# A decoder trunk on one core: the second feed-forward matrix set between whole blocks of the first, and weight buffers handed on by age

## The chip, the cores and the metric

The kernel runs on one core of a Trainium2 chip. The metric is the device time of one execution in microseconds (us). Before the change it was 2306.26 us, the median of three runs from 2303.05 to 2313.5 us.

## What is computed

The reference is a trunk of two layers on 512 tokens of width 1024. Each layer projects the normalised input once (`h @ w_in`), runs four causal token mixers on pieces of it, gates and sums their outputs, and then does this:

```
x  = x + mixed @ w_out
h2 = rms_norm(x, norm_ff)
x  = x + square(relu(h2 @ w_ff1)) @ w_ff2
```

`w_out` is 1024 x 1024, `w_ff1` 1024 x 4096 and `w_ff2` 4096 x 1024. The change lies in these three lines and in the buffers that their weights pass through. All matmuls read float32 data as a pair of a rounded part and a remainder, three matmuls for each product.

## The kernel before, in words

**Stages.** For each layer `mix` runs the four mixers in an order written out by hand, and `feed` runs the three lines above: first the output projection (eight weight chunks, in `OUT_ORDER`), then `factors`, which prepares the normalised input, then the feed-forward part.

**Blocks.** The hidden width of 4096 is cut into eight blocks of 512, n = 0 to 7. Each block is a 2 x 2 product done with seven products in place of eight (Strassen and Winograd). Its weights are four loaded quarters, "11", "21", "22" and "12" (512 KB each), and four sums of them that DVE makes: s3 = 21 + 11, s1 = 21 + 22 (written over 21), s2 = s3 + 22 and s4 = s2 + 12. Each of the seven weights 11, s3, s2, 12, s1, s4, 22 is then split: ACT copies it to a rounded tile, and DVE subtracts the copy and writes the remainder in place. `quarters` traces all this. One product is 24 matmuls of 256 columns. Its order on the tensor engine (PE), as traced, is 11; then s4 and 22 of the block before (`finish`, which also squares the hidden values); then s3, s2, 12, s1. So the last two products of a block lie in the block after it.

**Groups of the second matrix.** `down` multiplies the hidden values of two blocks by eight chunks of `w_ff2` (m = 0 to 7, 24 matmuls of 512 columns each, 512 KB each). It is called inside blocks 2, 4 and 6, after `finish`, and once more behind block 7. The first two chunks are begun with half of their matmuls each (`first`), since the hidden values of the second block come late.

**Weight buffers.** `chunk` and `quarters` load into 4 KB-per-partition buffers that hold the raw weight and later its remainder. `mix` uses three of them, wr0 to wr2, in turn (`dual("wr")`). `feed` uses nine: these three and ww3 to ww8, which share memory with the mixers' tiles `yl` and `e`. They stand in a list, `wfree`: `take` pops its head, `drop` appends a buffer behind the last product that reads it. Both happen while the program is traced, so which buffer a load gets is fixed by program order, and at run time the load waits until the last reader of that buffer is done. A block holds seven of the nine. The list lives on from one layer to the next.

**Tiles for the rounded copies.** `wh` has two slots and serves the chunks and the weights s3 and s1 of a block; `fh` has three and serves 11, s2, 12, s4 and 22. The hidden values take `fx`, eight slots, four for each block.

**What sets the order.** A planner puts the instructions of each engine into a fixed order at compile time: by priority, each as soon as the planner's own model says that it is ready. Loads, sums and splits of weights are traced at a priority 2000 instructions ahead of their place (`high_priority(2000)`), evacuations of blocks 4000 ahead. All weight loads are issued on SP's queue, which works in order.

The lines that the steps of the prediction touch are the split on lines 580 to 584, the sums on lines 589 to 598, the loads on lines 577 (quarters) and 301 (chunks), the split of a chunk on lines 305 and 306, and the copies of the mixers' sum on lines 497 and 498.

Of the kernel before, what the change touches and what calls it, by code (L numbers as in the profile page):

```python
# [10 lines left out]
F32R = mybir.dt.float32r  # L11
# [33 lines left out]
def fb(ap):  # L45
    return ap.bitcast(F32)


class Dual:
# [5 lines left out]
    @property  # L55
    def f(self):
        assert self.live
        return self._f
# [6 lines left out]
class Kern:  # L65
# [50 lines left out]
    def take(self):  # L116

        b = self.wfree.pop(0)
        if b[2] is not None:
            b[2].live = False  # L120
        b[2] = Dual(b[0], b[1])
        b[2].home = b
        return b[2]

    def drop(self, d):
        d.live = False
        self.wfree.append(d.home)
# [318 lines left out]

    def mix(self, l, x):
        nc = self.nc
        self.l = l
        if l > 0:  # L450
            self.load_small(l)
        self.hh, self.hl = self.norm_split(x, self.sp(l, C_GMIX, 8))

        p0 = self.tc.cur_priority
        acc = [self.vproducts("s") for _ in range(2)]
        with self.tc.high_priority(self.tc.cur_priority - p0):
            self.rb, self.rt = self.rms(x, "d", l == 0)
        if l == 0:
            self.setup_more()
        else:  # L460
            for k in range(KT):
                nc.sync.dma_start(self.xs[:, k, :], x[k][:])
        for c in range(2):
            self.sb_v(c, acc[c])
        self.dtag = "d"
        self.mixed, self.begun = None, set()
        self.y, self.Ab, self.st, self.cd, self.gg, self.V = {}, [None] * 4, {}, {}, {}, {}
        gens = {}
        for it in MIXERS:
            f = getattr(self, it[0])  # L470
            if it[0] in STEPS:
                g = gens.get(it[:-1])
                if g is None:
                    g = gens[it[:-1]] = f(*it[1:-1])
                next(g, None)
            else:
                f(*it[1:])
        assert all(next(g, self) is self for g in gens.values())
# [9 lines left out]

    def feed(self, l):
        nc = self.nc  # L490
        X2 = lambda tiles: lambda k: tiles[k // 2][:, (k % 2) * S:(k % 2) * S + S]
        HH, HL = [], []
        for k in range(0, KT, 2):
            hh, hl = self.t("fx", 1024, F32R), self.t("fx", 1024, F32R)
            for i in range(2):
                h = slice(i * S, i * S + S)
                nc.scalar.activation(hh[:, h], self.mixed[k + i][:], AF.Copy)
                nc.vector.tensor_sub(hl[:, h], self.mixed[k + i][:], fb(hh[:, h]))
            HH.append(hh)
            HL.append(hl)  # L500
        x = self.load_x(self.A["x"] if l == 0 else self.xs)
        for m in OUT_ORDER:
            wh, wl = self.chunk(wide=True)
            o = self.ps("d")
            self.halves(wh, wl, X2(HH), X2(HL), o[:], range(KT))
            self.drop(wl)
            with self.hi():
                nc.vector.tensor_add(x[m][:], x[m][:], o[:])
        F = self.factors(x, self.sp(l, C_GFF, 8))
        pend, hid = None, []  # L510
        for n in range(8):
            W = self.quarters()
            s = dict(W=W, X=self.ps("s"), H=hid)
            self.product(s["X"], W["11"], F["11"], True)
            s["e1"] = self.taken(s["X"])
            if pend:
                self.finish(pend, F)
            if n > 0 and n % 2 == 0:
                self.down(x, hid[:4], None)
                del hid[:4]  # L520
            if n == 1:
                ms, rs = self.square_norm(x)
                for k in range(KT):
                    nc.vector.tensor_mul(x[k][:], x[k][:], ms[:])
            if n == 0:
                s["Z"] = self.ps("s")
                self.product(s["Z"], W["12"], F["21"], True)
            s["Y"] = self.ps("s")
            self.product(s["Y"], W["s3"], F["3"], True)
            self.product(s["X"], W["s2"], F["2"], False)  # L530
            s["e2"] = self.taken(s["X"])
            if n > 0:
                s["Z"] = self.ps("s")
                self.product(s["Z"], W["12"], F["21"], True)
            s["ra"], s["rb"] = self.t("rl", 1024), self.t("rl", 1024)
            with self.evac():
                nc.vector.tensor_add(s["ra"][:, 0:S], s["Z"][:], s["e1"][:])
                nc.scalar.activation(s["ra"][:, 0:S], s["ra"][:, 0:S], AF.Relu)
            self.product(s["X"], W["s1"], F["1"], False)
            with self.evac():  # L540
                e3 = self.taken(s["Y"])
                nc.vector.tensor_add(s["rb"][:, S:], s["X"][:], e3[:])
            pend = s
        self.down(x, hid, rs, pend, F, l == self.depth - 1)
        return x
# [23 lines left out]
    def quarters(self):  # L569

        nc = self.nc
        q, out = {}, {}
        add = nc.vector.tensor_add

        def load(n):
            q[n] = self.take()
            nc.sync.dma_start(q[n].f[:], self.A["w"][self.cidx])
            self.cidx += 1

        def split(n):  # L580
            wh = self.t("wh" if n in ("s3", "s1") else "fh", 1024, F32R)
            nc.scalar.activation(wh[:], q[n].f[:], AF.Copy)  # L582
            nc.vector.tensor_sub(q[n][:], q[n].f[:], fb(wh[:]))
            out[n] = wh, q[n]
        with self.tc.high_priority(2000):
            for n in QUARTERS[:3]:
                load(n)
            q["s3"] = self.take()
            add(q["s3"].f[:], q["21"].f[:], q["11"].f[:])
            split("11")  # L590
            q["s1"] = q["21"]
            add(q["s1"].f[:], q["21"].f[:], q["22"].f[:])
            q["s2"] = self.take()
            add(q["s2"].f[:], q["s3"].f[:], q["22"].f[:])
            split("s3")
            load("12")
            q["s4"] = self.take()
            add(q["s4"].f[:], q["s2"].f[:], q["12"].f[:])
            for n in ("s2", "12", "s1", "s4", "22"):
                split(n)  # L600
        return out

    def factors(self, x, gcol):

# [858 lines left out]
def _kxm(w, c0):  # L1463

    k = w.shape[0] // P
    return w[:, c0:c0 + P].reshape(k, P, P).transpose(1, 0, 2).reshape(P, k * P)
# [11 lines left out]
QUARTERS = ("11", "21", "22", "12")  # L1478
# [21 lines left out]
def weight_stream(inp, l):  # L1500
    w = inp["w_in"][l]
    out = []
# [35 lines left out]
    for m in OUT_ORDER:  # L1538
        out.append(_kxm(inp["w_out"][l], m * P))

    def quarters(n):
        for q in QUARTERS:
            i, j = int(q[0]) - 1, int(q[1]) - 1
            c = n * 512 + i * 256
            out.append(inp["w_ff1"][l][j * 512:(j + 1) * 512, c:c + 256].reshape(4, P, 256).transpose(1, 0, 2)
                       .reshape(P, 1024))
    for n in range(9):
        if n < 8:
            quarters(n)
        if n > 0 and n % 2 == 0:  # L1550
            g = n // 2 - 1
            for m in (0, 2, 1, 3, 4, 5, 6, 7) if n == 8 else range(8):
                out.append(_kxm(inp["w_ff2"][l][g * 1024:(g + 1) * 1024], m * P))
    return out


# [74 lines left out]
```

## Time and profile before

| | us |
|---|---|
| median of three runs | 2306.26 |
| lowest and highest | 2303.05, 2313.5 |
| the profiled execution | 2308.0 |
| its span, first to last instruction | 2306.3 |
| around the span | 1.7 |
| PE busy in the span | 2219.8 (96%) |
| DVE busy | 1638.6 (71%) |
| ACT busy | 1148.0 (50%) |

The profiled execution lies 1.7 us above the median and inside the range of the runs. Layer 0's `feed` runs from about 736 to 1154 us of the span, layer 1's from about 1876 us to the end. The share of busy time of PE says little by itself, since matmuls overlap and a slow one counts as busy; what counts is how many matmuls a stretch holds.

### The profile page before, as it was taken

The page shows a single profiled execution, that of the slowest core. Times are in us where ns is not written, and L with a number is a line of the kernel's source. Part 1 is how long each engine was busy: PE and PEld are TensorE (multiplying, and loading weights), DVE is VectorE, ACT ScalarE, POOL GpSimd, SP SyncE. Part 2 cuts the span into 40 slices and gives each one's busy share as a digit, 9 for nine tenths or more (in the row PEclk, how much of TensorE's full clock was granted, in tenths as well). Part 3 has the DMA queues.
Part 4 walks back from the last instruction along what each step waited for, and adds up shares of the span by engine and source line. Part 5 has one row for each costly group of instructions (what it writes and reads, how often), then busy time and mean ns, then how long its engine had stood idle before and what let it go on. Part 6 is the DMA issues. An engine that isn't in the chain of part 4 may idle for free.

```text
span 2306.3 us, 31559 instructions
## 1 busy us (share of the span) xinstructions
PE 2219.8 (96%) x11896; PEld 1876.3 (81%) x11896; DVE 1638.6 (71%) x2577; ACT 1148.0 (50%) x1773; POOL 398.6 (17%) x743
## 2 busy tenths in 40 slices
PE   8999999998998999999999999999989999999997
PEld 7888888886787898887888888788768878988886
DVE  6889597888864775464558886878888558663645
ACT  5775444445444553353447654434455446442433
POOL 1223124433111000000112220334431110000000
PEclk9999999999899999999999999999989999999999
DMA  4222223321124122223222222223211342223231
GB/s 164 77 72 74 83 74 96 124 85 55 55 92 146 65 93 92 96 88 103 103 95 70 70 70 90 73 96 122 78 55 57 102 143 74 101 83 110 76 108 46
DMA packets 63119, 204.91 MB, mean 89 GB/s; under 512 B 7496, under 2 KB 10184, under 8 KB 62968
## 3 DMA queue, kind: packets, MB, share of 16 engines
q1 hardware_dynamic: 62968, 202.90, 26.7%
q8 instruction: 95, 1.56, 0.3%
q14 instruction: 56, 0.46, 0.1%
HBM read 198.57 MB, written 4.29 MB: 88 GB/s over the span
## 4 chain that ended last, share of the span: by engine, by line
PE 87%; DVE 7%; ACT 2%; DMA 2%; issue 1%; POOL 1%; POOLq 0%; DVEq 0%; SPq 0%; ACTq 0%
PE pd L147 60%; PE ps L147 26%; PE ps L975 1%; DMA wr0f<-in_w 1%; DVE wr1r L306 0%; ACT fh L582 0%; ACT wh L582 0%; DMA ww7f<-in_w 0%; POOL sm L858 0%; DVE sh L1089 0%; DVE wr0r L306 0%; ACT wh L305 0%; DVE fx L674 0%; DVE Q L861 0%; DMA wr2f<-in_w 0%
## 5 line engine op out<-in xcount | busy, mean ns | idle before, releaser
L147 PE MATMUL pd<-hh,wh 128*128 128x512 f32 x1040 | 416.0, 400 | 0.8 <-DVE gt L407 0.8
L147 PE MATMUL pd<-fx,wh 128*128 128x512 f32 (+1 forms) x1264 | 400.2, 394 | 12.4 <-ACT wh L305 12.3
L147 PE MATMUL pd<-hl,wh 128*128 128x512 f32 x1040 | 411.0, 395 | 0.0
L147 PEld LDWEIGHTS pd<-fx,wh 128*128 128x128 f32 x1264 | 238.4, 190 | 63.8 <-ACT wh L305 15.8
L147 PE MATMUL ps<-F,fh 128*128 128x256 f32 x1280 | 246.7, 284 | 21.2 <-ACT fh L582 21.1
L147 PEld LDWEIGHTS pd<-hh,wh 128*128 128x128 f32 x1040 | 195.6, 188 | 45.7 <-issue 4.2
L147 PEld LDWEIGHTS pd<-hl,wh 128*128 128x128 f32 x1040 | 195.4, 188 | 41.9 <-issue 0.2
L147 PEld LDWEIGHTS ps<-F,fh 128*128 128x128 f32 x1280 | 205.5, 191 | 27.1 <-ACT fh L582 23.0
L726 DVE TENSOR_TENSOR x<-x,pd 128x512 f32<-128x512 f32 (+1 forms) x63 | 42.8, 679 | 192.4 <-PE pd L147 192.4
L305 ACT ACTIVATE wh<-wr0f 128x1024 fp32r<-128x1024 f32 x77 | 81.6, 1060 | 150.0 <-PE pd L147 128.6
L147 PE MATMUL pd<-hh,wr2r 128*128 128x512 f32 x392 | 154.2, 393 | 0.0
L305 ACT ACTIVATE wh<-wr2f 128x1024 fp32r<-128x1024 f32 x72 | 76.3, 1059 | 125.3 <-PE pd L147 106.0
L147 PE MATMUL pd<-hh,wr1r 128*128 128x512 f32 x336 | 132.7, 395 | 0.0
L305 ACT ACTIVATE wh<-wr1f 128x1024 fp32r<-128x1024 f32 x68 | 72.0, 1059 | 109.3 <-PE pd L147 85.8
L147 PE MATMUL pd<-hh,wr0r 128*128 128x512 f32 x312 | 122.8, 394 | 0.0
L147 PE MATMUL ps<-p,v 128*128 128x384 f32 (+3 forms) x384 | 116.2, 426 | 2.7 <-POOL p L878 2.7
L306 DVE TENSOR_TENSOR wr0r<-wr0f,wh 128x1024 fp32r<-128x1024 f32 x77 | 100.9, 1310 | 22.1 <-ACT wh L305 21.6
L147 PE MATMUL pd<-yh,wh 128*128 128x512 f32 x256 | 104.0, 406 | 9.9 <-ACT yh L737 9.1
L147 PE MATMUL ps<-F,wh 128*128 128x256 f32 x512 | 108.3, 299 | 3.2 <-ACT p L553 1.9
L878 POOL TENSOR_SCALAR_AFFINE_SELECT p<-p 128x128 f32<-128x128 f32 x192 | 81.7, 445 | 160.3 <-ACT p L877 158.7
L781 POOL TENSOR_TENSOR mixed<-mixed,gt 128x512 f32<-128x512 f32 x48 | 66.8, 1396 | 245.4 <-DVE gt L779 241.8
L306 DVE TENSOR_TENSOR wr2r<-wr2f,wh 128x1024 fp32r<-128x1024 f32 x72 | 96.3, 1338 | 12.3 <-ACT wh L305 11.8
(636 smaller groups left out, 5522.6 us busy)
## 6 DMA issues: line engine op xcount, KB each, us to landing
wr0f<-in_w SPq DMA_DIRECT2D x91, 512.0 KB, 3.4
wr1f<-in_w SPq DMA_DIRECT2D x84, 512.0 KB, 3.3
wr2f<-in_w SPq DMA_DIRECT2D x80, 512.0 KB, 3.3
ww7f<-in_w SPq DMA_DIRECT2D x22, 512.0 KB, 3.4
ww6f<-in_w SPq DMA_DIRECT2D x20, 512.0 KB, 3.4
ww3f<-in_w SPq DMA_DIRECT2D x18, 512.0 KB, 3.3
ww5f<-in_w SPq DMA_DIRECT2D x16, 512.0 KB, 3.4
ww8f<-in_w SPq DMA_DIRECT2D x13, 512.0 KB, 3.4
```

The source lines that it names most:

```text
L147: i = self.nc.tensor.matmul(o, l, r, start=start, stop=stop, skip_group_check=True)
L305: nc.scalar.activation(wh[:], raw.f[:], AF.Copy)
L306: nc.vector.tensor_sub(raw[:], raw.f[:], fb(wh[:]))
L726: nc.vector.tensor_add(x[m][:, h], x[m][:, h], o[:, 0:h.stop - h.start])
L781: nc.gpsimd.tensor_add(self.mixed[m][:], self.mixed[m][:], g)
L878: nc.gpsimd.affine_select(d[:, 0:P], d[:, 0:P], [[1, P]], OP.is_gt if strict else OP.is_ge, 0.0, base=0, channel_multiplier=-1)
L975: nc.tensor.transpose(S3[n][:, c:c + P], at(F, q)[:, j * P:(j + 1) * P], self.ident)
```

## The change

Four things change.

1. `quarters` becomes a generator in two parts. Part one loads 11, 21 and 22, makes s3 and s1 and splits 11. Part two makes s2, loads 12, makes s4 and splits the other six.
2. `down` moves. It is called in blocks 3, 5 and 7, between the two parts of `quarters`, before any product of the block; the last call behind block 7 stays. It reads the hidden values of the two blocks that ended before the block just past (in block 3: blocks 0 and 1). The order of the weights in memory follows.
3. The tiles of the rounded copies are dealt out in another way: `wh` serves s3, 12 and s4 beside the chunks, `fh` serves 11, s2, s1 and 22.
4. `widen`, at the start of `feed`, puts the three wr buffers at the head of the list, the one that `mix` used longest ago first. `narrow`, at the start of `mix`, lets `mix` begin its turn with the wr buffer that was freed first.

```diff
+    def narrow(self):
+        wr = [b for b in self.wfree if b in self.ring["wr"][1]]
+        self.ring["wr"] = [0, wr]
+    def widen(self):
+        n, wr = self.ring["wr"]
+        n %= len(wr)
+        self.wfree = wr[n:] + wr[:n] + [b for b in self.wfree if b not in wr]
...
     def mix(self, l, x):
         nc = self.nc
+        self.narrow()
...
     def feed(self, l):
         nc = self.nc
+        self.widen()
...
         for n in range(8):
-            W = self.quarters()
+            prep = self.quarters()
+            W = next(prep)
+            if n > 2 and n % 2:
+                self.down(x, hid[:4], None)
+                del hid[:4]
+            next(prep)
             s = dict(W=W, X=self.ps("s"), H=hid)
             self.product(s["X"], W["11"], F["11"], True)
             s["e1"] = self.taken(s["X"])
             if pend:
                 self.finish(pend, F)
-            if n > 0 and n % 2 == 0:
-                self.down(x, hid[:4], None)
-                del hid[:4]
...
-            wh = self.t("wh" if n in ("s3", "s1") else "fh", 1024, F32R)
+            wh = self.t("wh" if n in ("s3", "12", "s4") else "fh", 1024, F32R)
...
             add(q["s1"].f[:], q["21"].f[:], q["22"].f[:])
+        yield out
+        with self.tc.high_priority(2000):
             q["s2"] = self.take()
             add(q["s2"].f[:], q["s3"].f[:], q["22"].f[:])
-            split("s3")
             load("12")
             q["s4"] = self.take()
             add(q["s4"].f[:], q["s2"].f[:], q["12"].f[:])
-            for n in ("s2", "12", "s1", "s4", "22"):
+            for n in ("s3", "s2", "12", "s1", "s4", "22"):
                 split(n)
-        return out
+        yield out
```

The function that lays out the weights in memory puts quarters 11, 21, 22 ahead of a group of `w_ff2` and quarter 12 behind it, in blocks 3, 5 and 7.

## Rows read from the trace of the kernel before

**Rows 1.** The page: engines' shares of the chain that ended last.

```profile
PE 87%; DVE 7%; ACT 2%; DMA 2%; issue 1%; POOL 1%; POOLq 0%; DVEq 0%; SPq 0%; ACTq 0%
```

**Rows 2.** PE's waits over the span: total us, times, longest us.

```profile
PE ps L147 <- ACT fh L582: 21.1, 9, 4.8
PE pd L147 <- ACT wh L305: 12.3, 7, 6.6
```

**Rows 3.** Windows of 20 us: busy us and instructions per engine, PE's granted clock.

```profile
807.00:827.00 20.00, 20.00 (x170) 20.00 (x169) 18.39 (x21) 14.79 (x18) 0.00 (x0) 1.00 0.31 103
...
899.00:919.00 20.00, 16.02 (x105) 15.19 (x104) 16.49 (x16) 8.30 (x11) 0.00 (x0) 0.83 0.17 53
990.50:1010.50 20.00, 16.09 (x119) 15.52 (x118) 17.42 (x17) 12.09 (x14) 0.00 (x0) 0.91 0.27 93
1081.50:1101.50 20.00, 16.03 (x112) 15.32 (x113) 14.24 (x14) 8.27 (x11) 0.00 (x0) 0.91 0.38 122
2036.50:2056.50 20.00, 15.72 (x112) 15.04 (x112) 17.34 (x17) 9.24 (x12) 0.00 (x0) 0.91 0.21 63
2127.00:2147.00 20.00, 14.62 (x100) 14.12 (x99) 15.85 (x15) 10.73 (x13) 0.00 (x0) 0.83 0.23 79
2219.50:2239.50 20.00, 15.99 (x117) 15.30 (x116) 15.10 (x14) 11.87 (x14) 0.00 (x0) 0.91 0.43 139
```

**Rows 4.** The chain of waits behind block 4's group: start us, us, what.

```profile
985.12 5.10 PE pd L147 x23
990.22 3.35 DMA ww5f<-in_w
...
993.59 1.23 DVE ww8f L592
...
997.09 1.15 DVE ww4r L583
...
998.28 29.88 PE ps L147 x234
```

**Rows 5.** SP's timeline in block 2's group: issues of block 3's quarters.

```profile
846.44 0.33 SPq L577 DMA_DIRECT2D ww3f<-in_w  x1
...
887.83 0.33 SPq L577 DMA_DIRECT2D ww8f<-in_w  x1
...
898.82 0.33 SPq L577 DMA_DIRECT2D wr0f<-in_w  x1
```

**Rows 6.** The two seams from `mix` to `feed`: windows, columns as in rows 3.

```profile
735.90:762.00 26.10, 19.38 (x72) 15.34 (x72) 9.38 (x11) 8.27 (x11) 1.57 (x1) 0.80 0.37 131
1876.50:1900.00 23.50, 19.16 (x73) 15.27 (x74) 9.51 (x12) 8.22 (x11) 1.58 (x1) 0.85 0.40 145
```

**Rows 7.** SP's timeline at layer 0's seam, chunk loads into wr buffers.

```profile
724.75 0.33 SPq L301 DMA_DIRECT2D wr1f<-in_w  x1
...
735.74 0.33 SPq L301 DMA_DIRECT2D wr0f<-in_w  x1
```

**Rows 8.** The chain of waits at layer 1's seam.

```profile
1879.06 0.43 ACT fx L497
...
1879.59 2.00 ACT wh L305 x2
```

**Rows 9.** The chain in layer 0's output projection: one chunk.

```profile
780.18 5.50 PE pd L147 x24
```

**Rows 10.** SP's timeline there: the load of block 0's quarter 22.

```profile
756.92 0.33 SPq L577 DMA_DIRECT2D wr1f<-in_w  x1
```

**Rows 11.** ACT's timeline there: splits of a chunk, of s2, of quarter 22.

```profile
762.65 1.06 ACT L305 ACTIVATE wh<-ww4f 128x1024 fp32r<-128x1024 f32 x1 [3.09 <-PE pd L147]
...
769.17 1.06 ACT L582 ACTIVATE fh<-ww3f 128x1024 fp32r<-128x1024 f32 x1
...
797.66 1.06 ACT L582 ACTIVATE fh<-wr1f 128x1024 fp32r<-128x1024 f32 x1
```

**Rows 12.** A window inside block 4's group, columns as in rows 3.

```profile
947.00:987.00 40.00, 40.00 (x195) 33.56 (x194) 13.34 (x15) 9.26 (x9) 0.00 (x0) 1.00 0.30 99
```

More of the change, by code (lines that the diff above doesn't have):

```diff
@@ L1539, in weight_stream, with quarters @@
         out.append(_kxm(inp["w_out"][l], m * P))
-    def quarters(n):
-        for q in QUARTERS:
+    def quarters(n, qs):
+        for q in qs:
             i, j = int(q[0]) - 1, int(q[1]) - 1
@@ L1548, in weight_stream @@
         if n < 8:
-            quarters(n)
-        if n > 0 and n % 2 == 0:
+            quarters(n, QUARTERS[:3])
+        if n > 2 and (n % 2 or n == 8):
             g = n // 2 - 1
@@ L1553, in weight_stream @@
                 out.append(_kxm(inp["w_ff2"][l][g * 1024:(g + 1) * 1024], m * P))
+        if n < 8:
+            quarters(n, QUARTERS[3:])
     return out
```

## The prediction, made before the change was run

> **What bounds the kernel now.** I read the page's chain first: 87% of it is PE [rows 1], so time comes from making PE stand still less or run faster, not from fewer instructions elsewhere. Then PE's waits: its two largest groups are waits for a split weight, behind ACT's copy on line 582 (a quarter) and line 305 (a chunk) [rows 2]. Those lie in the feed-forward stage and at its start. So I went through that stage in windows. Where nothing is wrong, 20 us hold 170 matmuls of 256 columns at the full granted clock [rows 3]. Behind each of the six groups of `w_ff2` that lie inside the blocks (three in each layer), a window of the same length holds only 105, 119, 112, 112, 100 and 117 [rows 3]. The reader should see two things in these rows: the missing matmuls, and a granted clock of 0.83 to 0.91. [...]
>
> The chain behind one group says why [rows 4]. The group's last chunk ends at 990.22. At that moment, and no sooner, a quarter of the next block is issued; it lands after 3.35 us, then DVE adds, splits, and the steady row of matmuls begins at 998.28. The load is late because of the list of buffers, not because of the queue: block 3's four quarters go out at 846.44, 887.83, 898.82 and one between the last two [rows 5]. These three are 5.5 us apart, which is just one chunk's time on PE [rows 9]. When `quarters(3)` is traced, the head of `wfree` holds the three buffers through which the eight chunks were passed in turn, so 11, 21 and 22, which everything else in the block rests on, wait for the chunks' last readers. Quarter 12, needed last, got a buffer that had long been free, and went out 41 us sooner. Nothing is left to cover the wait: the planner has by then used up the last two products of the block before, which are traced behind 11, as fill inside the group: 40 us inside a group hold 195 matmuls [rows 12], where chunks alone would be 40 / 0.229 = 175 (0.229 us is 5.50 us over 24 [rows 9]).
>
> The second place is the seam from the mixers to the output projection. From the mixers' last matmul, 26.1 us hold 72 matmuls of 512 columns in layer 0, 23.5 us hold 73 in layer 1 [rows 6]. In layer 0 the three wr buffers come free 5.5 us apart, wr1 at 724.75 and wr0 last, at 735.74 [rows 7], and the first chunk was given wr0. In layer 1 the first chunk sits in ww7, mixer memory, and its split stands on ACT behind the last copy of `mixed` [rows 8].
>
> **What the change takes away.** Groups: at full pace six windows would hold 6 x 170 = 1020 matmuls; they hold 665. The 355 missing ones are 355 x 20 / 170 = 41.8 us. Seams, at 0.229 us a matmul: layer 0, 26.1 - 72 x 0.229 = 9.6 us; layer 1, 23.5 - 73 x 0.229 = 6.8 us. Together 16.4. All in all at most 58.2 us.
>
> **What becomes of the groups, followed through the list.** In block 2 the list is empty once all seven weights are taken. Behind it come, in order of their drops, the buffers of 11, of block 1's s4 and 22, then s3, s2, 12 and s1 of block 2. Part one of `quarters(3)` takes the first four, all free before the group starts. The chunks get the other three in turn (s2's, 12's, s1's). Part two gets them back: s2 the sixth chunk's buffer, free two chunks (11 us) before the group ends, quarter 12 the seventh's, 5.5 us before, s4 the last. Quarter 12 thus lands 5.5 - 3.35 = 2.1 us before the end. Its `wh` slot may come from the last chunk; then 1.06 us on ACT [rows 11] and 1.23 on DVE [rows 4] make it ready 2.3 us behind the group. Ahead of it PE has s3 and s2, 24 matmuls each, 2.8 us by the steady pace, 5.6 us in all. On ACT and DVE the hidden values of the block before come first, since `fx` is full until the group ends: two copies and two subtractions, 2 x 1.23 on DVE behind the first copy. That makes 4.7 us instead of 2.3, still under 5.6. So the stall at the end goes. What is late next is s4, which is not needed until the next block.
>
> At the group's start the first chunk's load waits for s2, lands 3.35 us later and is split in 2.3: 5.6 us, while 12 and s1 run 5.6. The fill, should it be late, is 11 of block 3, and s4 and 22 of block 2: three products of 2.8 us, 8.5 in all, that are ready. The second chunk needs a `wh` slot while s4 and the first chunk hold both; when the planner runs out of chunk work it has to run s4, which frees one. Its split (2.3 us) lies under 22 (2.8). Inside a group PE is full now with 3 buffers and 2 slots [rows 12], and stays so. I take 0.5 us for each group, 3 us, as what small waits remain; the ends are 0 and the second rival's price.
>
> **Seams.** Layer 0's first chunk gets wr1, free 11 us before the mixers end, and a `wh` slot with the second to last chunk of `mix`, 5.5 us before; its split takes 2.3. Layer 1 is the same with its oldest wr buffer. What could take over is `mixed`: its last tile is copied from 1879.06 on [rows 8]; copy and subtraction of 512 columns take half of a split's 1.06 and 1.23 us by estimate, so it is there at about 1880.3. It feeds the last three of the first chunk's 24 matmuls, due 21 x 0.229 = 4.8 us after the chunk begins at 1876.5, so at 1881.3. I take 0.5 us each, 1 us; ends 0 and 2 us each, should it come late.
>
> **Edits costed near nothing.** Matmuls, loads and splits are the same in number; each is only moved, on SP's queue past the chunks' loads as well. Quarter 12 of block 0 now waits for a `wh` slot of the last output chunk (it had `fh`), and s1 moves to `fh`. ACT at the end of the projection does one copy for the other, 1.06 us. Cover: 11 of block 0 runs for about as long; without it up to 2.3 us a layer. I take 0.5 each, 1 us. `narrow` only turns the names: `mix` of layer 1 starts on buffers that are released one by one before the layer begins, as now. DVE is the engine to watch, 18.39 of 20 us in steady blocks [rows 3], but there PE is already full.
>
> Sum: 2308.0 (span 2306.3 and 1.7 around it) - 58.2 + 3 + 1 + 1 = 2254.8. The profiled execution stands 1.7 us over the median, so I forecast **2253 us** for the median.
>
> **Rivals.**
> First, the change does only half of what it says: the planner again pulls 11, s3 and s2 of the next block into the group as fill, and quarter 12 is missed just as 22 is now. The fill in today's order [rows 12] speaks for it; against it that 12 now goes out one chunk before the end and that s2 cannot be used before the sixth chunk. Then only the seams gain: 2308 - 16.4 + 2 = 2293, 2292 for the median.
>
> Second, the stall moves to the group's start: ACT works in order, and the second chunk's split stands at its head until s4 is done, with evacuations behind it. One split shows, 2.3 us, and the lower clock behind it; at the layer 0 seam 9.6 us were lost, and PE's longest wait behind line 305 was 6.6 [rows 2], so a factor of 1.45: 3.3 us, times six, 20 us: 2273. ACT's waits for PE before a chunk's split [rows 11] speak for it, the 8.5 us of fill against it. [...]
>
> Third, slower: s3 of the next block, ready early, takes one of the two `wh` slots before the chunks do. Its remainder may not be written until s2's sum has read it, and that waits for the sixth chunk's buffer. The chunks then pass through one slot, and five of them show 2.3 x 1.45 = 3.3 us each, 16.5 a group, 99 in all: 2253 + 99 = 2352; 8.5 us of fill a group, 51 in all, bring it down to about 2300. It decides from 58.2 / 6 = 9.7 us a group, that is three chunks that show. Against it: block 0's quarter 22 is issued at 756.92 [rows 10], so it is there at about 760.3; ACT stood idle for 3.09 us before 762.65 [rows 11], and of the three `fh` slots only 11's was in use, since s2, the next in traced order, is copied at 769.17; yet 22 is split at 797.66, behind all those traced ahead of it. Slots are handed out in traced order, and the chunks come before s3.
>
> **Chances.** My forecast 0.68, from 2242 (all 58.2 us, and small waits elsewhere that the new dealing of slots may take) to 2264 (seams and quarter 12 late by their upper ends). The second rival 0.15, 2264 to 2285. The first 0.09, 2285 to 2297. The third 0.05, 2300 to 2352; the rest, 0.03, no change by other accidents of the planner's order. 0.5% is 11.5 us, about what a measurement can tell: faster means under 2294.7. Faster 0.68 + 0.15 + 0.07 = 0.90; same 0.05; slower 0.05. The range that leaves out 2 in 10 is 2242 to 2279.
>
> **What would show it.** Windows of 20 us behind the groups in blocks 3, 5 and 7 hold about 165 matmuls with the clock at 1.0. On SP, 11, 21 and 22 of the next block go out before the group's first chunks, and 12 one chunk before its end. At the seams PE goes on within 1 us, and the first chunk reads the wr buffer that came free first. I am wrong if PE waits for line 305 inside a group (second and third), if it still waits for line 582 behind one (first), or if the mixers of layer 1 lengthen.

## The result, and the profile after

| | before | after |
|---|---|---|
| median, us (4 runs each) | 2304.66 | 2249.05 |
| lowest and highest | 2300.51, 2313.5 | 2247.02, 2251.93 |
| the profiled execution | 2308.0 | 2247.0 |
| its span | 2306.3 | 2245.3 |

The four runs before are the three above and one more. The ratio is 0.9755, with a 95% interval from 0.9723 to 0.9786: faster by 55.6 us. The forecast was 2253.

Where the time came from is seen by cutting both spans at the ends of the mixers and of the feed-forward stages; the four pieces fill each span:

| stretch, us | before | after | difference |
|---|---|---|---|
| mixers of layer 0 | 736.0 | 733.0 | -3.0 |
| `feed` of layer 0 | 418.1 | 388.85 | -29.25 |
| mixers of layer 1 | 722.4 | 720.35 | -2.05 |
| `feed` of layer 1 | 429.8 | 403.1 | -26.7 |

The two `feed` stages give 55.95 us, close to the difference of the medians, 55.6. The 5.05 us in the mixers make up the rest of the 61.0 us between the two profiled executions. The first 3 us can be placed: in the windows of the first microseconds, before anything that the change touches, the kernel before shows a granted clock of 0.91 and 131 matmuls from 10 to 30 us, and the kernel after 1.00 and 141. The experiment e7_tail, whose mixers are traced as in the kernel after, shows 0.91 and 130 there, and its mixers of layer 0 end at 735.8 us, as in the kernel before. So these 3 us go with the execution and not with the change. The 2.05 us in layer 1 can't be put down to the change either: in e7_tail those mixers take 722.7 us, as in the kernel before, and in e10_free 720.2.

The page's chain after, engine shares (87% was PE in [rows 1]):

```profile
PE 90%; DVE 6%; ACT 1%; issue 1%; DMA 1%; POOL 1%; SPq 0%; POOLq 0%; DVEq 0%; ACTq 0%
```

PE's waits after, as in [rows 2] (total us, times, longest us). Line 315 is the split of a chunk, line 597 now that of a quarter:

```profile
PE pd L157 <- ACT yh L752: 9.5, 4, 3.1
...
PE ps L157 <- ACT wh L315: 2.2, 4, 0.8
PE ps L157 <- ACT p L567: 1.9, 2, 0.9
PE pd L157 <- ACT wh L315: 1.3, 4, 0.4
```

The 21.1 us behind a quarter's split are gone from the list. Behind a chunk's copy there were 13.3 us, the 12.3 in [rows 2] and 1.0 in a row of their own; 3.5 remain, in short pieces. None of it lies in the six groups: from the first chunk's load to the row of matmuls behind the last chunk, PE shows no wait at all in any of them. The largest group that is left, behind line 752, stood in the list before with 9.1 us in four waits.

The windows that answer to [rows 3], 20 us behind each of the six groups:

```profile
888.50:908.50 20.00, 20.00 (x169) 19.93 (x169) 15.47 (x15) 9.16 (x12) 0.00 (x0) 1.00 0.16 54
972.60:992.60 20.00, 20.00 (x169) 19.92 (x169) 15.49 (x15) 9.14 (x12) 0.00 (x0) 1.00 0.15 54
1056.70:1076.70 20.00, 19.89 (x156) 19.09 (x154) 7.82 (x9) 5.69 (x8) 0.00 (x0) 1.00 0.33 106
1997.90:2017.90 20.00, 20.00 (x169) 19.93 (x168) 15.45 (x16) 9.17 (x12) 0.00 (x0) 1.00 0.16 53
2082.00:2102.00 20.00, 20.00 (x169) 19.93 (x168) 15.46 (x16) 9.17 (x12) 0.00 (x0) 1.00 0.17 53
2166.10:2186.10 20.00, 19.85 (x155) 19.05 (x153) 7.81 (x9) 5.73 (x8) 0.00 (x0) 1.00 0.34 108
```

Four windows hold 169, where 100 to 119 stood, with the clock at 1.00 throughout. The third and the sixth, behind block 7's group, already hold the last group's matmuls of 512 columns, so fewer matmuls fill the same time there: PE is busy for 19.89 and 19.85 of the 20 us.

SP's timeline around block 3's group, which answers to [rows 5]; line 591 loads a quarter, line 311 a chunk:

```profile
818.76 0.33 SPq L591 DMA_DIRECT2D ww6f<-in_w  x1
819.72 0.33 SPq L591 DMA_DIRECT2D ww8f<-in_w  x1
826.15 0.33 SPq L591 DMA_DIRECT2D wr1f<-in_w  x1
829.96 0.33 SPq L311 DMA_DIRECT2D wr0f<-in_w  x1
...
871.66 0.33 SPq L311 DMA_DIRECT2D ww3f<-in_w  x1
882.65 14.62 SPq L591 DMA_DIRECT2D wr0f<-in_w  x2
```

Block 3's 11, 21 and 22 go out from 818.76 on, ahead of the first chunk, and 12 at 882.65 (the first of the two in that row). The chain shows the end of the group with no other engine between PE's two rows:

```profile
885.95 2.52 PE pd L157 x11
888.47 11.54 PE ps L157 x96
```

Quarter 12 is issued 5.8 us before 888.47, about one chunk (5.50 us in [rows 9]). In [rows 4], 8.06 us lie between the end of the chunks and the row of matmuls that follows.

The two seams, windows as in [rows 6], and SP's chunk loads at the first, as in [rows 7]:

```profile
733.00:759.10 26.10, 26.10 (x118) 21.47 (x117) 18.21 (x19) 13.06 (x17) 1.61 (x1) 1.00 0.37 132
1842.20:1865.70 23.50, 23.50 (x107) 19.34 (x106) 15.79 (x17) 9.43 (x13) 1.61 (x1) 1.00 0.42 149
```

```profile
721.89 0.33 SPq L311 DMA_DIRECT2D wr1f<-in_w  x1
727.38 0.33 SPq L311 DMA_DIRECT2D wr2f<-in_w  x1
...
732.88 0.33 SPq L311 DMA_DIRECT2D wr0f<-in_w  x1
```

PE is busy for the whole of both windows, with 118 and 107 matmuls in place of 72 and 73. The first chunk's load now is that of wr1, 11.1 us before the mixers end at 733.0.

### The profile page after: what moved, and what is told of

It reads as the page before. It is cut to its first block, busy times and chain, and to the rows that moved or that the text cites. A ratio compares the mean times of both kernels' runs of the same rounds, so it can differ in the third digit from the quotient of the medians.

```text
span 2245.3 us, 31549 instructions
## 1 busy us (share of the span) xinstructions
PE 2194.9 (98%) x11896; PEld 1859.2 (83%) x11896; DVE 1639.3 (73%) x2577; ACT 1145.4 (51%) x1773; POOL 398.3 (18%) x743
## 4 chain that ended last, share of the span: by engine, by line
PE 90%; DVE 6%; ACT 1%; issue 1%; DMA 1%; POOL 1%; SPq 0%; POOLq 0%; DVEq 0%; ACTq 0%
PE pd L157 62%; PE ps L157 27%; PE ps L990 1%; DVE wr1r L316 0%; POOL sm L873 0%; ACT F L637 0%; DMA wr0f<-in_w 0%; DVE sh L1104 0%; DVE Q L876 0%; DVE wr0r L316 0%; DVE wr2r L316 0%; DVE m L1474 0%; DMA wr2f<-in_w 0%; DVE m L851 0%; DVE sx L869 0%
## 5 line engine op out<-in xcount | busy, mean ns | idle before, releaser
L157 PE MATMUL pd<-fx,wh 128*128 128x512 f32 (+1 forms) x1264 | 393.4, 390 | 1.3 <-ACT wh L315 1.3
L157 PE MATMUL ps<-F,fh 128*128 128x256 f32 x1024 | 194.4, 283 | 1.9 <-ACT p L567 1.9
L157 PEld LDWEIGHTS ps<-F,fh 128*128 128x128 f32 x1024 | 163.2, 191 | 3.1 <-ACT p L567 2.3
L157 PE MATMUL pd<-hh,wr1r 128*128 128x512 f32 x416 | 164.4, 395 | 0.0
L157 PE MATMUL ps<-F,wh 128*128 128x256 f32 x768 | 144.4, 282 | 0.6 <-DVE F L638 0.6
L157 PEld LDWEIGHTS ps<-F,wh 128*128 128x128 f32 x768 | 121.0, 188 | 2.9 <-issue 1.4
L157 PE MATMUL pd<-hh,wr2r 128*128 128x512 f32 x312 | 123.0, 394 | 0.0
```

The lines of the kernel that those rows point to most:

```text
L157: i = self.nc.tensor.matmul(o, l, r, start=start, stop=stop, skip_group_check=True)
```

## The experiments

Gains and losses against the kernel before go by its median in the same runs (2302.99 to 2303.38 us). Losses against the kernel after compare two sets of runs; the medians of the kernel before in these sets differ by 1.7 us at most. The experiments stand in the order of the argument.

| kernel | median, us | ratio to before, 95% interval |
|---|---|---|
| e1_seam | 2289.71 | 0.9942 [0.9927, 0.9957] |
| e2_groups | 2273.93 | 0.9869 [0.9851, 0.9887] |
| e3_early | 2252.33 | 0.978 [0.9764, 0.9796] |
| e5_whole | 2249.89 | 0.9768 [0.9754, 0.9783] |
| e6_late | 2285.98 | 0.9929 [0.9902, 0.9956] |
| e4_slots | 2249.4 | 0.9762 [0.9746, 0.9778] |
| e7_tail | 2249.28 | 0.9759 [0.9745, 0.9774] |
| e8_held | 2428.32 | 1.0542 [1.0524, 1.056] |
| e9_last | 2282.1 | 0.9906 [0.9891, 0.992] |
| e10_free | 2249.49 | 0.9768 [0.9753, 0.9782] |

### The two parts apart

**e1_seam** is the kernel before with `widen` and `narrow` alone.

```diff
     def mix(self, l, x):
         nc = self.nc
+        self.narrow()
...
     def feed(self, l):
         nc = self.nc
+        self.widen()
```

> The kernel before with widen and narrow alone. My theory: the two seams are worth 16.4 us less small waits, and the six groups keep all their 41.8 us: about 2289 us, ratio 0.993. Rival (the seams are hidden anyway, by the mixers' last sum or by later waits): no change, ratio 1.000, the time comes back before the output projection ends.

It gained 13.6 us (9.9 to 16.8 by the interval). The seams' term, 16.4 less the 1 us kept back, lies inside. The two calls were never run apart, so what `narrow` does alone isn't shown.

**e2_groups** is the kernel after without these two calls.

```diff
-        self.narrow()
...
-        self.widen()
```

> The changed kernel without widen and narrow. My theory: the parts add up, so the groups' 41.8 us go and the seams' 16.4 stay: 2263 us, ratio 0.982 (0.980 to 0.985). Rival (the seam's gain depends on the rest): within 4 us of the changed kernel, 2253 us, ratio 0.978.

It lost 24.9 us against the kernel after, more than the term of 16.4, and came out 11 us above the 2263 expected; against the kernel before it gained 29.1. The chain at layer 1's seam shows where some of it lies:

```profile
1847.86 8.94 PE pd L157 x39
...
1856.95 6.40 DMA ww8f<-in_w
...
1864.40 1.05 ACT wh L315
...
1865.49 4.52 PE pd L157 x11
```

The new order of the groups also leaves the list in another order at the end of layer 0, and it then begins with ww8, mixer memory that comes free last. Its load is issued only at 1856.95 and takes 6.40 us, its split another 1.05, and the chain leaves PE at 1856.80 and comes back at 1865.49, 8.7 us later. So the parts don't add: the two calls are worth 13.6 us in the old order and 24.9 in the new one.

### Which part of the move the groups' gain comes from

The prediction laid the stalls to late buffers. The rival reading is that the place of the group, or beginning the next block ahead of it, is what pays. Three kernels separate these. **e3_early** leaves the groups, the undivided `quarters` and the slots as before, has `widen` and `narrow`, and only turns the list, so that the quarters get buffers that have long been free and the chunks' buffers go to the back.

```diff
         for n in range(8):
+            if n > 2 and n % 2:
+                self.wfree = self.wfree[3:] + self.wfree[:3]
             W = self.quarters()
```

> widen and narrow, the groups at their old place, and the list turned by three ahead of the quarters of blocks 3, 5 and 7, so that 11, 21 and 22 get the buffers that the block before freed early and s2, 12 and s4 those of the chunks. My theory (the stall comes from late buffers, the place is only a means): most of the 41.8 us goes, 2250 to 2262 us, ratio 0.977 to 0.982. Rival (the place pays, since 11, s4 and 22 are traced behind the group as cover): little more than the seams, 2280 to 2290 us, ratio 0.990 or more.

**e5_whole** has the groups in the new place, but all of `quarters` behind them, so that nothing is begun ahead.

```diff
-            prep = self.quarters()
-            W = next(prep)
             if n > 2 and n % 2:
                 self.down(x, hid[:4], None)
                 del hid[:4]
+            prep = self.quarters()
+            W = next(prep)
             next(prep)
```

> The changed kernel, but the quarters of blocks 3, 5 and 7 traced in one piece behind the group, so that no load of the next block is traced ahead of it. The chunks then pass through the buffers of 11, s4 and 22, and 11, 21, 22 get those of s3, s2 and 12. My theory: these are free early all the same, so the time stays within 5 us of the changed kernel, about 2250 us, ratio 0.976. Rival (it is the next block's beginning ahead of the group that pays): the groups' stalls come back, 2280 to 2290 us, ratio 0.990.

**e6_late** is e5_whole with the list turned the other way: 11, 21 and 22 get the three buffers that the chunks used.

```diff
                 del hid[:4]
+                self.wfree = self.wfree[-3:] + self.wfree[:-3]
+            prep = self.quarters()
```

> As the kernel with the quarters in one piece behind the group, and the list turned so that 11, 21 and 22 get the chunks' three buffers again, as in the kernel before. My theory: the stalls come back, all of them (2291 us, ratio 0.993) if the planner spends s4 and 22 of the block before inside the group, a quarter of them (2260 us, ratio 0.980) if it leaves them as cover behind it. Rival (the place alone pays): no different from the changed kernel, about 2250 us, ratio 0.976.

With the seams mended in all four:

| median, us | quarters in the chunks' buffers | quarters in older buffers |
|---|---|---|
| old place of the group | 2289.71 (e1_seam) | 2252.33 (e3_early) |
| new place | 2285.98 (e6_late) | 2249.89 (e5_whole) |

The columns differ by 37.4 and 36.1 us, the rows by 3.7 and 2.4, which is little beside the runs of e6_late (2279.56 to 2294.95). e5_whole and the kernel after (2249.05) can't be told apart. The buffers' age makes the gain; the place and the early start add at most a few microseconds. SP's timeline of e6_late shows the cause in its old form, at the pace of the chunks, 5.5 us apart:

```profile
872.51 0.33 SPq L592 DMA_DIRECT2D ww3f<-in_w  x1
878.01 0.33 SPq L592 DMA_DIRECT2D ww5f<-in_w  x1
883.50 0.33 SPq L592 DMA_DIRECT2D ww6f<-in_w  x1
```

and its chain what follows from the last of them, issued at the group's end, as in [rows 4]:

```profile
867.91 15.59 PE pd L157 x69
883.50 3.19 DMA ww6f<-in_w
...
887.86 1.22 DVE ww5f L607
...
891.40 8.68 PE ps L157 x58
```

### Slots for the rounded copies

**e4_slots** deals out `wh` and `fh` as before.

```diff
-            wh = self.t("wh" if n in ("s3", "12", "s4") else "fh", 1024, F32R)
+            wh = self.t("wh" if n in ("s3", "s1") else "fh", 1024, F32R)
```

> The changed kernel with the rounded copies dealt out as before: wh for s3 and s1, fh for 11, s2, 12, s4 and 22. My theory: the slots are worth next to nothing, block 0 and the last group shift by 1 to 2 us each way: 2245 to 2253 us, ratio 0.975 to 0.978. Rival (the new dealing is needed, since five copies a block through three slots come too late behind a group): waits for line 596 behind the groups, 2260 us or more, ratio 0.981.

No difference (2249.4 against 2249.05): the new dealing costs and brings nothing that can be measured. **e7_tail** is about the one wait that the dealing brought. Behind block 7's group, s4 holds a `wh` slot and the last group's second chunk is split late; the chain after shows it:

```profile
1076.29 1.06 ACT wh L315
...
1077.38 1.24 DVE ww3r L316
...
1078.65 2.79 PE ps L157 x11
```

```diff
-            wh = self.t("wh" if n in ("s3", "12", "s4") else "fh", 1024, F32R)
+            wh = self.t("wh" if n in ("s3", "12", "s4")[:2 + (not last)] else "fh", 1024, F32R)
```

(`last` is true in block 7.)

> The changed kernel, with s4 of block 7 alone back in fh. In the profile after, the third chunk of the last group waits for the wh slot that this s4 holds, 1.6 us in each layer, which the kernel before did not show. My theory: this wait goes, 2 to 3 us in all, ratio 0.1% below that of the changed kernel, 2246 us, to be seen in the trace rather than in the times. Rival (the wait is the hidden values' own): the wait stays or moves by as much, no change.

PE's waits in e7_tail hold 1.0 us of the 2.2 behind line 315 in the row of the kernel after, and two rows of 0.8 us behind a chunk's remainder (line 316) are gone:

```profile
PE ps L157 <- ACT wh L315: 1.0, 2, 0.8
```

and a window over the place in layer 0 is full:

```profile
1056.00:1080.00 24.00, 24.00 (x174) 22.69 (x173) 13.38 (x14) 9.91 (x13) 0.00 (x0) 1.00 0.30 105
```

The two gaps were 0.81 and 0.77 us in each layer, 3.2 us in all. In the profiled executions the two `feed` stages of e7_tail are 2.5 us shorter together than those of the kernel after. The median, 2249.28 us in five runs, doesn't show it: the mixers of layer 0 alone end anywhere from 731.3 to 738.6 us in the profiles of these experiments.

### The slower rival, made to happen

**e8_held** lets s3 take its `wh` slot ahead of the group and keep it, as the third rival has it: its copy is traced in part one, its subtraction behind the sum s4 in part two.

```diff
             add(q["s1"].f[:], q["21"].f[:], q["22"].f[:])
+            held = self.t("wh", 1024, F32R)
+            nc.scalar.activation(held[:], q["s3"].f[:], AF.Copy)
         yield out
...
-            for n in ("s3", "s2", "12", "s1", "s4", "22"):
+            nc.vector.tensor_sub(q["s3"][:], q["s3"].f[:], fb(held[:]))
+            out["s3"] = held, q["s3"]
+            for n in ("s2", "12", "s1", "s4", "22"):
```

> The changed kernel, with s3 of the next block copied in part one, ahead of the group: its wh slot is then dealt out before those of the chunks, and its remainder still waits for s2's sum. This is the third rival of the prediction, forced. By its price: the chunks go through one slot until s3's product is done, PE waits behind line 315, five waits of 2.3 us and the lower clock, less the fill: 2300 us, up to 2352, ratio 0.998 or more. Rival (the planner runs s3's product or others early enough and hides it): 2250 to 2265 us, ratio 0.976 to 0.983.

It lost 179.3 us against the kernel after, 29.9 a group. PE's waits name the chunk's split, 42 times, seven for each group, and then a quarter's remainder:

```profile
PE pd L157 <- ACT wh L315: 45.1, 42, 1.3
...
PE ps L157 <- DVE ww7r L597: 7.5, 2, 3.8
```

The chain inside the group shows one chunk behind the other, with copy and subtraction between them in full:

```profile
854.15 1.07 ACT wh L315
...
855.24 1.24 DVE ww3r L316
...
856.52 7.16 PE pd L157 x23
```

The mechanism is real, then, and its price was put too low: 16.5 us a group in the prediction. Five chunks were to show; seven did. Behind the chunks a quarter's remainder shows once a group, 3.6 to 3.8 us each under four buffers' names, the first time that of s2. And no fill made up for it: in block 3's group PE runs the chunks' matmuls alone from 847 to 900 us. At 2428.32 us it lies outside the 2300 to 2352 expected.

### The cover behind the group

The prediction held that quarter 12 may land late, since PE has s3 and s2, 5.6 us, ahead of it. **e9_last** tests this: 12 gets the last chunk's buffer and s4 the one before.

```diff
                 del hid[:4]
+                f = self.wfree
+                f[1], f[2] = f[2], f[1]
             next(prep)
```

> The changed kernel, but quarter 12 gets the last chunk's buffer in place of the one before, and s4 that one: 12 is issued 5.5 us later, when the group ends. The working of the prediction: it lands 3.35 us behind the group and is split in 2.3, so it is ready 5.7 us behind; PE has s3 and s2 before it, 5.6 us. So 0 to 1 us a group, 2249 to 2256 us, ratio 0.976 to 0.979. Rival (there was no such cover, and the buffer one chunk sooner is what keeps PE going): the old wait of 3 to 4 us a group and the lower clock, 2275 us or more, ratio 0.987.

The cover didn't hold: 33 us lost against the kernel after, 5.5 a group. In e9_last the load of 12 is issued at 889.46, when the group ends: one chunk later than 882.65, in an execution that runs some 1.2 us behind that of the kernel after at this place. DVE's timeline behind the group:

```profile
892.80 1.23 DVE L615 TENSOR_TENSOR wr0f<-ww5f,ww3f 128x1024 f32<-128x1024 f32 x1 [2.42 <-DMA ww3f<-in_w]
893.94 1.22 DVE L605 TENSOR_TENSOR ww4f<-ww7f,ww6f 128x1024 f32<-128x1024 f32 x1
895.08 1.22 DVE L599 TENSOR_TENSOR ww5r<-ww5f,fh 128x1024 fp32r<-128x1024 f32 x1
```

and PE's, the two matmuls ahead of which it waits:

```profile
893.92 0.39 PE L157 MATMUL ps<-F,wh 128*128 128x256 f32 x1 [1.44 <-ACT wh L598]
...
896.35 0.39 PE L157 MATMUL ps<-F,ww5r 128*128 128x256 f32 x1 [2.04 <-DVE ww5r L599]
```

The first DVE row is the sum s4 = s2 + 12, the third the subtraction that writes s2's remainder over s2 (ww5); between them DVE makes a sum of block 4. The sum s4 must have read s2 before s2 is overwritten. So s2, PE's second product, waits for 12 as well, through a buffer that is both summed from and written in place: 2.04 us. The 1.44 us ahead of that are a wait for 12's own copy, the only copy into `wh` that ACT makes between the group's end and that matmul; the planner has set one matmul of 12 ahead of s2's remainder. The window from there on divides the loss:

```profile
889.50:909.50 20.00, 16.52 (x123) 16.11 (x122) 14.50 (x14) 6.98 (x9) 0.00 (x0) 0.91 0.16 53
```

47 matmuls are missing from 170, 5.5 us. PE stood idle for 3.48 of it, the sum of its two waits; the mean granted clock of 0.91 over 20 us takes another 1.8.

**e10_free** keeps e9_last's late 12 and breaks the tie: in blocks 3, 5 and 7, s4 is begun as s3 + 22, s3 and s2 are split, and only then 12 is added. With s2 free of 12, the planner also sets the matmul of 12 behind s2.

```diff
+            if early:
+                add(q["s4"].f[:], q["s3"].f[:], q["22"].f[:])
+                split("s3")
+                split("s2")
+                add(q["s4"].f[:], q["s4"].f[:], q["12"].f[:])
```

> The kernel in which quarter 12 gets the last chunk's buffer, with one thing added in blocks 3, 5 and 7: s4 is begun as s3 + 22, a second sum of what s2 holds, and 12 is added to it behind the split of s2. So s2's remainder, which overwrites s2 in place, no longer waits for s4's sum, and that for the landing of 12; DVE has one addition more, 1.2 us a block. My theory now (s2's split was tied to the landing of 12 through s4's sum): the 33 us that the late quarter cost go but for 0 to 1 us a group, 2249 to 2258 us, ratio 0.976 to 0.980. Rival (12 itself comes too late for its own product, or the queue on DVE is what holds): 2270 us or more, ratio 0.985.

2249.49 us: all of it comes back, with 12 issued at 889.31. DVE's timeline in e10_free still has the wait for the load, 1.97 us against 2.42, with nothing of the next two products behind it:

```profile
892.62 1.23 DVE L619 TENSOR_TENSOR wr0f<-wr0f,ww3f 128x1024 f32<-128x1024 f32 x1 [1.97 <-DMA ww3f<-in_w]
```

Now s3 and s2 do cover it: 12's remainder is ready at 895.18, and PE reads it at 895.23, behind both, after a wait of 0.2 us. So the prediction's sum for a late 12 holds once the tie is gone.

The tie is there in the kernel after too. Its DVE timeline:

```profile
888.28 1.23 DVE L613 TENSOR_TENSOR ww3f<-ww5f,wr0f 128x1024 f32<-128x1024 f32 x1 [0.42 <-PE pd L157]
...
890.02 1.22 DVE L597 TENSOR_TENSOR ww5r<-ww5f,fh 128x1024 fp32r<-128x1024 f32 x1
891.15 1.22 DVE L597 TENSOR_TENSOR wr0r<-wr0f,wh 128x1024 fp32r<-128x1024 f32 x1
```

and the first matmuls on PE that read the remainders of s2 (ww5) and 12 (wr0):

```profile
891.29 0.39 PE L157 MATMUL ps<-F,ww5r 128*128 128x256 f32 x1
...
894.15 0.28 PE L157 MATMUL ps<-F,wr0r 128*128 128x256 f32 x1
```

The sum s4 begins as soon as the last chunk gives up ww3. Quarter 12, the one that the prediction watched, is ready at 892.37 and read at 894.15: 1.8 us to spare, where the prediction had 5.6 less 4.7. s2's remainder has nothing to spare. It is there at 891.24 and PE reads it at 891.29, when s3 is done. The same 0.05 us lie between DVE's end and PE's start in e9_last (896.30 and 896.35), where PE did wait, and 0.05 to 0.06 behind the other three comparable groups. So it just fits, and what it hangs on is s4's buffer, freed by the last chunk, not 12's.

## Why the prediction was right

**What bounded the kernel.** Right. Late buffers, not SP's queue and not the place of the group, made the stalls: the same group at the same place costs 36 to 37 us by the choice of its buffers alone, and the load at 898.82 in [rows 5] went out 0.03 us behind the last matmul that read its buffer (898.40 and 0.39 us).

**The groups' term, 41.8 less 3.** Right. From e1_seam to e5_whole, which adds the groups' part to the seams', it is 39.8 us.

**The seams' term, 16.4 less 1.** Right in the old order of the list (13.6, from 9.9 to 16.8). The two terms were added as if each stood alone, and e2_groups shows that they don't: without the two calls the groups' part gains 29.1 us, not 39.8, since what the calls repair depends on the order in which the groups leave the list. The sum came out because the change has both.

**The residuals, 5 us.** By layer, the missing matmuls came to 30.1 and 28.1 us (20.5 and 21.3 for the groups, 9.6 and 6.8 for the seams); `feed` became shorter by 29.25 and 26.7. So 2.25 us came back, not 5. Nothing of it lies in the groups, where 3 had been put: PE has no wait there, and the four comparable windows hold 169 of 170. Both seam windows are full too. The part that can be named is the tail of the last group, 1.6 us in each layer, which the prediction didn't have; that makes 3.2, so the count of missing matmuls is good to about 1 us. Of the 4 us by which the forecast lies above the median, 2.75 are these residuals.

**The step that failed.** "Ahead of it PE has s3 and s2" was wrong as the price of a late quarter 12. s3 alone is cover; s2 is tied to 12 by s4's sum, and the planner sets a matmul of 12 ahead of it (e9_last; e10_free undoes both at once, so their shares, 2.04 and 1.44 us of idle time, are read from the trace alone). "What is late next is s4, which is not needed until the next block" fails for the same reason: s4's product is not needed, but its sum is, since s2's remainder is written behind it. In the change 12 lands in time and the error didn't show. That it didn't is partly luck: the tie of s2 to s4's sum wasn't counted, and it fits with nothing to spare. With 12 one chunk later it is worth 33 us.

**The slots** were costed at nothing, and e4_slots agrees.

**The rivals.** The first (fill pulled in, 12 missed) didn't occur: no wait for a quarter's split is left behind a group. Nor did the second: its 20 us would stand inside the groups, and PE has no wait there. ACT does stand 4.43 us, waiting for PE, ahead of a chunk's split at 860.91, inside block 3's group, and PE still runs on, since that split's 2.3 us then lie under the other chunk's 5.5. In e8_held the chunks have one slot left, so no other chunk runs meanwhile, and PE pays: 45.1 us in 42 waits behind a chunk's copy. The third rival was rightly given little: slots are dealt out in traced order, and the chunks had theirs first. Its price was too low by nearly half.

What stays open: how the 33 us of e9_last divide between s2's tie and the early matmul of 12, and what `narrow` does alone.

## What to carry to other kernels

When prefetch buffers come from a list that is fixed at trace time, read the issue times on the queue first: loads that go out one chunk apart, each as a chunk ends, got their buffers from those chunks. Giving them older buffers (two lines, e3_early) was worth nearly as much as setting the stage in a new order. When you count what covers a late load, follow every sum that reads it and every buffer that such a sum reads and that is later written in place: the work behind those is no cover.

## What the runs showed that was not expected

A window roughly divides a loss by itself: PE's idle time, and (1 - granted clock) times its length. For the first group in [rows 3] that is 3.98 us and 3.4 us, together 7.4, against 65 missing matmuls, 7.6 us (the clock's part shows by itself in the kernel before from 909.2 to 912.6 us: granted 0.50, PE busy throughout, 18 matmuls; in the kernel after the same 3.4 us have 1.00 and 31); for all six groups 25.5 and 14.0, together 39.5 against 41.8; for e9_last 3.48 and 1.8 against 5.5. A few short waits are thus dear. In e9_last two waits of 1.44 and 2.04 us cost 5.5, and in e8_held waits of about 2 us between chunks bring a window at full stretch down to this, at a mean granted clock of 0.91:

```profile
846.00:902.00 56.00, 42.51 (x150) 30.84 (x150) 14.90 (x16) 12.73 (x14) 0.00 (x0) 0.91 0.21 66
```

13.5 us of 56 are idle, and the clock takes 5.0 more.
